# Gate rows as one-hots in pairs of tokens: one VectorE comparison for two keys, scaled copies on ScalarE

## The chip, the cores and the metric

The kernel runs on one core of a Trainium2 chip. The metric is the device time of one execution in microseconds; the median of three runs is compared. A second number, the span, is the time from the first to the last instruction in one profiled execution.

## The reference, cut to what matters

The program is a transformer block on 256 tokens of width 1024 with convolution, window attention and a "peer" layer, and after it two more layers with attention and feed-forward parts. The change lies in the peer layer alone:

```python
s_top, i_top = lax.top_k(sc, PEER_TOPK)              # 8 heads, two key sets of 128, top 16 of each
...
best, pos = lax.top_k(cand, PEER_TOPK)               # 16 of the 256 pairs, for each head
expert_idx = jnp.take_along_axis(cand_idx, pos, axis=-1)
gate = jax.nn.softmax(best, axis=-1).astype(h.dtype)
...
a = jax.nn.gelu(jnp.einsum("ced,cd->ce", u_emb[idx], hx), approximate=False)
return jnp.einsum("ce,ced->cd", g * a, v_emb[idx])
```

So each token has 8 x 16 = 128 experts out of 128 x 128. Expert (i, j) is row 128 i + j of two tables of 16384 rows and 1024 columns: its activation is the gelu of the row of the first table with the token, and the gate times that weighs the row of the second table.

## The kernel before, in words

The peer layer treats the tokens in two ways at the same time (`ROWS`, lines 80 to 81 of the kernel). The last 96 tokens are done by fetching rows. Each of 96 steps for a table fetches 128 rows of 4 KB by an indirect DMA on GpSimd's queue (`RowGroup.row`, L1555, six buffers `row`), and VectorE consumes the rows in its queue's order: a product with sum for the first table (`RowGroup.dot`, L1560, 96 times), a scaled addition for the second (`RowGroup.axpy`, L1568 and L1570, 96 times).

The first `N` = 160 tokens are done densely. For each of the 128 values of i, `ublock` loads a block of 512 KB of the first table (tiles `raw`, `whi` and `wlo`, a ring of ten buffers, by SyncE's queue, L966), TensorE multiplies it with the tokens (L976), and ScalarE writes the gelu into `G[j, i, token]` (two tiles of 64 i each). The gates have to be multiplied into `G`. For that `onehots` (L992 to L997) makes rows for `NT` = 4 tokens at a time: `Q` is one where the slot's j is the column, `O` where its i is; `P` and `R` are `O` times the high and the low part of the gate, in half precision. `place` (L1009) multiplies `Q` with `P` and `R` on TensorE, which gives the 128 x 128 table of gates of one token, eight matmuls for four tokens. VectorE multiplies this table into those parts of `G` that exist already (L1015); ScalarE writes it into the parts whose gelu comes later (L1017), and these are multiplied when their u block is done (L982, L984, L985).

The 40 groups begin after 48 of the 128 u blocks; between two placements stand two u blocks, and rows are stepped along at the rate of `some_rows`. When all u blocks and placements are through, the v phase takes 128 blocks of 512 KB of the second table through the same ring and multiplies them with `G` (L1064), first those of the second `G` tile. `add` puts in the rows' sums near the end.

Nobody writes down the order in which the engines' instructions stand: a scheduler places each engine's queue by its own estimate of durations and dependences, and then every engine runs its queue in order. So where a row operation, a comparison and a product stand relative to each other on VectorE is the scheduler's choice. The stage begins at about 457 us and its u phase ends at about 705 us.

In the program, two lines of the loop over groups tie the rows to the u blocks:

```python
ublock(i, 4 * done)
some_rows(rate)
```

Of the kernel before, what the change touches and what calls it, by code (L numbers as in the profile page):

```python
# [9 lines left out]
F32 = mybir.dt.float32  # L10
F32R = mybir.dt.float32r
F16 = mybir.dt.float16
I32 = mybir.dt.int32
U32 = mybir.dt.uint32
AF = mybir.ActivationFunctionType
ALU = mybir.AluOpType
# [4 lines left out]
T = 256  # L21
# [51 lines left out]
UP = 2.0  # L73

NT = 4
RG = 0
G_SCALE = 2.0 ** 15


# [6 lines left out]
class Kernel:  # L86
# [710 lines left out]
    def peer(self):  # L797
        nc, a = self.nc, self.a
# [2 lines left out]
        park = self.dr.tile([128, C, T], F32, name="park")  # L801
        nc.gpsimd.dma_start(park, x)
        hn = p2h.tile([128, C, T], F32, name="hn")
        iT = p2h.tile([128, T], F16, name="iT")
        jT = p2h.tile([128, T], F16, name="jT")

        gT = p2h.tile([128, T], F32, name="gT")
        gTh = p2h.tile([128, T], F16, name="gTh")
        gTl = p2h.tile([128, T], F16, name="gTl")
        sk = p2q.tile([128, 16, 128], F32, name="sk")  # L810
        nc.gpsimd.dma_start(sk, a["subk"])
        isel = p2t.tile([128, 2, 8, 16], F32, name="isel")
# [96 lines left out]
        for h in range(8):  # L909
            for c in range(2):  # L910
                pt = self.chunk(xs)
# [11 lines left out]
        def gates():  # L923
            nc.vector.scalar_tensor_tensor(ei, isel, float(N_KEYS), jsel, op0=ALU.mult, op1=ALU.add)
            nc.vector.tensor_tensor(ex, best, best[:, :, :, 0:1].to_broadcast([128, 2, 8, 16]), op=ALU.subtract)
            nc.scalar.activation(ex, ex, AF.Exp)
            sm = p2t.tile([128, 2, 8], F32, name="sm", bufs=1)
            nc.vector.reduce_sum(sm, ex, axis=AX.X)
            nc.vector.reciprocal(sm, sm)
            nc.vector.tensor_mul(ex, ex, sm[:, :, :, None].to_broadcast([128, 2, 8, 16]))  # L930

            def turn():
                for n, src in enumerate((isel, jsel, ex)):
                    pt = self.pp.tile([128, T], F32, name="ax", bufs=4)
                    for tt in range(2):
                        nc.tensor.transpose(pt[:, tt * 128:(tt + 1) * 128], src[:, tt].rearrange("p a b -> p (a b)"), self.ident)
                    nc.scalar.activation((iT, jT, gT)[n], pt, AF.Copy, scale=(1.0, 1.0, G_SCALE)[n])
                self.split(gT, gTh, gT)
                nc.scalar.activation(gTl, gT, AF.Copy)
                for g in rows:  # L940
                    g.indices()
            self.later(1, turn)
# [43 lines left out]

        def onehots(t0, oh, io):

            ts = slice(t0, t0 + NT)
            Q, O, P, R = (oh.tile([128, 128, NT], F16, name=n, bufs=2) for n in ("Q", "O", "P", "R"))  # L990
            col = lambda v: v[:, None, ts].to_broadcast([128, 128, NT])
            nc.vector.tensor_tensor(Q, io, col(jT), op=ALU.is_equal)  # L992
            nc.vector.tensor_tensor(O, io, col(iT), op=ALU.is_equal)
            nc.vector.tensor_mul(P, O, col(gTh))
            if t0 >= RG:
                for k in range(NT):
                    nc.scalar.activation(R[:, :, k], O[:, :, k], AF.Copy, scale=gT[:, t0 + k:t0 + k + 1])  # L997
            else:
                nc.vector.tensor_mul(R, O, col(gTl))
            return Q, (P, R)  # L1000

        def place(t0, n_i, oh):

# [2 lines left out]
            for t in range(4):  # L1006
                for P in Ps:
                    k = (t0 + t) % NT
                    nc.tensor.matmul(pt[:, t], Q[:, :, k], P[:, :, k], start=P is Ps[0], stop=P is Ps[-1])  # L1009
            for k in range(2):  # L1010
                view = Gs[k][:, :, t0:t0 + 4].rearrange("p i t -> p t i")
                n = min(max(n_i - 64 * k, 0), 64)
# [18 lines left out]
        pgb = self.open("pgb", side="right")  # L1031
        Gs.append(pgb.tile([128, 64, N], F32, name="G1"))
        poh = self.open("poh", side="left")
        io = poh.tile([128, 128, NT], F16, name="io")
        nc.vector.tensor_copy(io, self.iota[:, :, None].to_broadcast([128, 128, NT]))
        i0 = i
        n_g = N // 4
        rate = fetch_steps() / (254.0 - i0)
# [739 lines left out]
```

## Time and profile before

| | us |
|---|---|
| median of three runs | 1668.67 |
| lowest and highest | 1668.29, 1671.47 |
| profiled execution | 1673.91 |
| its span | 1672.1 |
| TensorE busy | 1594.9 (95%) |
| VectorE busy | 1142.8 (68%) |
| ScalarE busy | 637.1 (38%) |
| GpSimd busy | 347.1 (21%) |
| mean DMA rate over the span | 239 GB/s |

Busy time is the time in which an engine has an instruction under way. TensorE's matmuls are pipelined, so its share says little about how near it is to its best. PE is TensorE's matmuls, PEld its weight loads, DVE VectorE, ACT ScalarE, POOL GpSimd, SP SyncE. What sets the time in a stage is read from the waits and windows of that stage, not from shares over the whole span.

### The profile page before, as it was taken

What the parts mean: (1) busy time and instruction counts of PE and PEld (TensorE: products, weight loads), DVE (VectorE), ACT (ScalarE), POOL (GpSimd) and SP (SyncE); (2) the same over time, 40 slices, a digit from 0 to 9 for tenths busy, and PEclk for the clock granted to TensorE, in tenths of its full rate; (3) what the DMA queues carried; (4) which work ended last, traced back from release to release, by engine and by line L of the source; (5) the groups of instructions that cost most, each with busy time, mean ns of one, the idle gap of its engine ahead of it and who ended that gap; (6) DMA issues with size and microseconds to landing.
All of it is one profiled execution on the core that took longest, in us unless ns stands there. A gap on an engine that the chain in (4) does not pass through costs nothing.

```text
span 1672.1 us, 29794 instructions
## 1 busy us (share of the span) xinstructions
PE 1594.9 (95%) x11502; PEld 1504.6 (90%) x11502; DVE 1142.8 (68%) x2599; ACT 637.1 (38%) x1373; POOL 347.1 (21%) x288
## 2 busy tenths in 40 slices
PE   8989989998989899899999999999999999999998
PEld 7878979998989899899888999887999998799986
DVE  7989978898178899854544007866776557676654
ACT  4557545531233343200000005455544445555443
POOL 3734630000045454543332000100000020000000
PEclk9989989999999999899999999999999999999999
DMA  5522437576799999999999865732755677365563
GB/s 184 171 80 93 137 123 228 160 252 198 239 402 406 408 381 409 395 409 409 409 409 409 317 196 159 246 102 87 224 185 182 186 189 211 94 188 183 180 189 113
DMA packets 109388, 398.97 MB, mean 239 GB/s; under 512 B 12484, under 2 KB 12643, under 8 KB 108736
## 3 DMA queue, kind: packets, MB, share of 16 engines
q1 hardware_dynamic: 78336, 282.63, 50.0%
q0 software_dynamic: 30768, 114.39, 18.1%
q8 instruction: 90, 1.47, 0.4%
q14 instruction: 50, 0.41, 0.1%
q10 hardware_dynamic: 144, 0.07, 0.0%
HBM read 394.86 MB, written 6.11 MB: 240 GB/s over the span
## 4 chain that ended last, share of the span: by engine, by line
PE 60%; DMA 19%; DVE 17%; issue 3%; ACT 1%; POOL 1%; SPq 0%; DVEq 0%; POOLq 0%; ACTq 0%
PE mm L145 12%; PE mm L146 11%; PE mm L147 11%; PE ax L1064 9%; DMA row<-un,idx 8%; DMA raw<-vv 4%; DMA whi<-vv 4%; PE mm L976 3%; DVE junk L1560 2%; DVE ax L589 2%; PE mm L213 1%; DVE wlo L126 1%; PE mm L211 1%; PE mm L212 1%; PE ax L442 1%
## 5 line engine op out<-in xcount | busy, mean ns | idle before, releaser
L122 ACT ACTIVATE whi<-raw 128x1024 fp32r<-128x1024 f32 x275 | 290.3, 1058 | 620.1 <-DMA raw<-wst 310.0
L126 DVE TENSOR_TENSOR wlo<-raw,whi 128x1024 fp32r<-128x1024 f32 x227 | 277.3, 1223 | 187.8 <-ACT whi L122 184.3
L145 PE MATMUL mm<-xgh,whi 128*128 128x256 f32 x1064 | 304.3, 286 | 0.0
L147 PE MATMUL mm<-xgh,wlo 128*128 128x256 f32 x1064 | 301.8, 284 | 0.4 <-DVE wlo L126 0.4
L146 PE MATMUL mm<-xgl,whi 128*128 128x256 f32 x1064 | 301.4, 283 | 0.0
L145 PEld LDWEIGHTS mm<-xgh,whi 128*128 128x128 f32 x1064 | 201.9, 190 | 1.1 <-issue 0.8
L147 PEld LDWEIGHTS mm<-xgh,wlo 128*128 128x128 f32 x1064 | 201.9, 190 | 0.7 <-DVE wlo L126 0.6
L146 PEld LDWEIGHTS mm<-xgl,whi 128*128 128x128 f32 x1064 | 202.0, 190 | 0.1
L1570 DVE SCALAR_TENSOR_TENSOR acc<-row,w,acc 128x1024 f32<-128x1024 f32 x94 | 120.7, 1284 | 111.1 <-DMA row<-vv,idx 111.0
L1555 POOL DMA_INDIRECT row<-un,idx x96 | 105.5, 1099 | 277.6 <-DVE idx L1550 169.4
L1560 DVE CUSTOM_DVE_ANT_0 junk<-row,h 128x1024 f32<-128x1024 f32 x96 | 117.5, 1224 | 33.9 <-DMA row<-un,idx 32.4
L124 POOL TENSOR_TENSOR wlo<-raw,whi 128x1024 fp32r<-128x1024 f32 x48 | 115.1, 2403 | 107.8 <-ACT whi L122 105.0
L1064 PE MATMUL ax<-G,raw 128*128 128x160 f32 x832 | 125.6, 303 | 3.1 <-DMA raw<-vv 1.0
L1555 POOL DMA_INDIRECT row<-vv,idx x96 | 96.7, 1008 | 142.8 <-DVE acc L1570 123.5
L1064 PEld LDWEIGHTS ax<-G,raw 128*128 128x128 f32 x832 | 116.1, 191 | 8.1 <-DMA raw<-vv 7.7
L976 PE MATMUL mm<-hn,raw 128*128 128x160 f32 x816 | 121.6, 304 | 0.1
L976 PEld LDWEIGHTS mm<-hn,raw 128*128 128x128 f32 x816 | 116.5, 195 | 0.4 <-ACT G L984 0.3
L146 PE MATMUL mm<-hl,whi 128*128 128x256 f32 x368 | 106.8, 290 | 2.2 <-DVE hl L356 2.1
L976 PE MATMUL mm<-hn,wlo 128*128 128x160 f32 x608 | 95.3, 313 | 5.0 <-ACT G L979 5.0
L589 DVE SCALAR_TENSOR_TENSOR ax<-u,cw,ax 128x256 f32<-128x256 f32 x227 | 97.7, 481 | 0.7
L1064 PE MATMUL ax<-G,wlo 128*128 128x160 f32 x608 | 93.6, 306 | 2.2 <-DMA wlo<-vv 0.6
L976 PEld LDWEIGHTS mm<-hn,wlo 128*128 128x128 f32 x608 | 90.5, 201 | 5.2 <-ACT G L979 5.2
(435 smaller groups left out, 3358.2 us busy)
## 6 DMA issues: line engine op xcount, KB each, us to landing
raw<-wst SPq DMA_DIRECT2D x278, 512.0 KB, 3.7
raw<-vv SPq DMA_DIRECT2D x52, 512.0 KB, 15.1
raw<-ut SPq DMA_DIRECT2D x51, 512.0 KB, 6.6
whi<-ut SPq DMA_DIRECT2D x39, 512.0 KB, 6.6
wlo<-ut SPq DMA_DIRECT2D x38, 512.0 KB, 6.7
wlo<-vv SPq DMA_DIRECT2D x38, 512.0 KB, 14.9
whi<-vv SPq DMA_DIRECT2D x38, 512.0 KB, 15.5
tabr<-tabd POOLq DMA_DIRECT2D x1, 2048.0 KB, 8.3
```

Source lines behind the costliest of these rows:

```text
L122: nc.scalar.activation(hi, raw, AF.Copy)
L124: nc.gpsimd.tensor_sub(lo, raw, hi)
L126: self.pin = nc.vector.tensor_sub(lo, raw, hi)
L145: nc.tensor.matmul(pt, w[:, s], xs[0][:, k], start=first, stop=False)
L146: nc.tensor.matmul(pt, w[:, s], xs[1][:, k], start=False, stop=False)
L147: nc.tensor.matmul(pt, lo[:, s], xs[0][:, k], start=False, stop=last)
L589: nc.vector.scalar_tensor_tensor(y[:, c] if k == 30 else ps, u[:, c, k:k + T], cw[:, c, k:k + 1], ps, op0=ALU.mult, op1=ALU.add)
L976: nc.tensor.matmul(pt, raw[:, k * 128:(k + 1) * 128], hn[:, k, :N], start=(k == 0), stop=(k == C - 1))
L1064: nc.tensor.matmul(acc[d // 2][:, d % 2, :N], raw[:, d * 128:(d + 1) * 128], G(i), start=False, stop=False, skip_group_check=True)
L1555: self.k.nc.gpsimd.indirect_dma_start(t, None, table, bass.IndirectOffsetOnAxis(ap=self.idx[:, s:s + 1], axis=0))
L1560: self.k.nc.vector.tensor_tensor_reduce(junk, row, self.h, 1.0, 0.0, ALU.mult, ALU.add, self.a[:, s:s + 1])
L1570: self.k.nc.vector.scalar_tensor_tensor(self.acc, row, w, self.acc, op0=ALU.mult, op1=ALU.add)
```

## The change

The tiles for the keys become one, `jiT`, with j and i beside each other. `Q` and `O` become one tile `QO` with both, laid out by pairs of tokens, in three buffers instead of two. One VectorE comparison makes both keys of two tokens, so two comparisons of 512 elements make a group, where two comparisons and one product of 512 elements did. `P` is no longer a VectorE product: it is a scaled copy on ScalarE for each token, as `R` is; `P` is scaled by the gate itself and rounded to half precision when written, `R` by what that rounding leaves, which is now kept in single precision (`gTl`, one ScalarE copy fewer). `io` shrinks from four tokens to two, and `place` reads the new layout.

```diff
--- before.py
+++ after.py
@@ -73,7 +73,6 @@
 UP = 2.0
 
 NT = 4
-RG = 0
 G_SCALE = 2.0 ** 15
 
 
@@ -801,12 +800,12 @@
         park = self.dr.tile([128, C, T], F32, name="park")
         nc.gpsimd.dma_start(park, x)
         hn = p2h.tile([128, C, T], F32, name="hn")
-        iT = p2h.tile([128, T], F16, name="iT")
-        jT = p2h.tile([128, T], F16, name="jT")
+
+        jiT = p2h.tile([128, 2, T], F16, name="jiT")
 
         gT = p2h.tile([128, T], F32, name="gT")
         gTh = p2h.tile([128, T], F16, name="gTh")
-        gTl = p2h.tile([128, T], F16, name="gTl")
+        gTl = p2h.tile([128, T], F32, name="gTl")
         sk = p2q.tile([128, 16, 128], F32, name="sk")
         nc.gpsimd.dma_start(sk, a["subk"])
         isel = p2t.tile([128, 2, 8, 16], F32, name="isel")
@@ -934,9 +933,8 @@
                     pt = self.pp.tile([128, T], F32, name="ax", bufs=4)
                     for tt in range(2):
                         nc.tensor.transpose(pt[:, tt * 128:(tt + 1) * 128], src[:, tt].rearrange("p a b -> p (a b)"), self.ident)
-                    nc.scalar.activation((iT, jT, gT)[n], pt, AF.Copy, scale=(1.0, 1.0, G_SCALE)[n])
-                self.split(gT, gTh, gT)
-                nc.scalar.activation(gTl, gT, AF.Copy)
+                    nc.scalar.activation((jiT[:, 1], jiT[:, 0], gT)[n], pt, AF.Copy, scale=(1.0, 1.0, G_SCALE)[n])
+                self.split(gT, gTh, gTl)
                 for g in rows:
                     g.indices()
             self.later(1, turn)
@@ -986,18 +984,17 @@
 
         def onehots(t0, oh, io):
 
-            ts = slice(t0, t0 + NT)
-            Q, O, P, R = (oh.tile([128, 128, NT], F16, name=n, bufs=2) for n in ("Q", "O", "P", "R"))
-            col = lambda v: v[:, None, ts].to_broadcast([128, 128, NT])
-            nc.vector.tensor_tensor(Q, io, col(jT), op=ALU.is_equal)
-            nc.vector.tensor_tensor(O, io, col(iT), op=ALU.is_equal)
-            nc.vector.tensor_mul(P, O, col(gTh))
-            if t0 >= RG:
-                for k in range(NT):
-                    nc.scalar.activation(R[:, :, k], O[:, :, k], AF.Copy, scale=gT[:, t0 + k:t0 + k + 1])
-            else:
-                nc.vector.tensor_mul(R, O, col(gTl))
-            return Q, (P, R)
+
+            QO = oh.tile([128, 2, NT // 2, 128, 2], F16, name="QO", bufs=3)
+            P, R = (oh.tile([128, NT // 2, 128, 2], F16, name=n, bufs=2) for n in ("P", "R"))
+            for p in range(NT // 2):
+                ps = slice(t0 + 2 * p, t0 + 2 * p + 2)
+                nc.vector.tensor_tensor(QO[:, :, p], io[:, None].to_broadcast([128, 2, 128, 2]),
+                                        jiT[:, :, None, ps].to_broadcast([128, 2, 128, 2]), op=ALU.is_equal)
+            for k in range(NT):
+                for dst, g in ((P, gT), (R, gTl)):
+                    nc.scalar.activation(dst[:, k // 2, :, k % 2], QO[:, 1, k // 2, :, k % 2], AF.Copy, scale=g[:, t0 + k:t0 + k + 1])
+            return QO[:, 0], (P, R)
 
         def place(t0, n_i, oh):
 
@@ -1006,7 +1003,7 @@
             for t in range(4):
                 for P in Ps:
                     k = (t0 + t) % NT
-                    nc.tensor.matmul(pt[:, t], Q[:, :, k], P[:, :, k], start=P is Ps[0], stop=P is Ps[-1])
+                    nc.tensor.matmul(pt[:, t], Q[:, k // 2, :, k % 2], P[:, k // 2, :, k % 2], start=P is Ps[0], stop=P is Ps[-1])
             for k in range(2):
                 view = Gs[k][:, :, t0:t0 + 4].rearrange("p i t -> p t i")
                 n = min(max(n_i - 64 * k, 0), 64)
@@ -1031,8 +1028,8 @@
         pgb = self.open("pgb", side="right")
         Gs.append(pgb.tile([128, 64, N], F32, name="G1"))
         poh = self.open("poh", side="left")
-        io = poh.tile([128, 128, NT], F16, name="io")
-        nc.vector.tensor_copy(io, self.iota[:, :, None].to_broadcast([128, 128, NT]))
+        io = poh.tile([128, 128, 2], F16, name="io")
+        nc.vector.tensor_copy(io, self.iota[:, :, None].to_broadcast([128, 128, 2]))
         i0 = i
         n_g = N // 4
         rate = fetch_steps() / (254.0 - i0)
```

The instructions stand in other places too. The first place is VectorE's queue in the middle of the stage, between the product of one group and that of the next (`G<-ax,G`; `ISA junk` is the product with sum of one fetched row, `ISA a` the short read of its sum). Before:

```order
L1015 SCALAR_TENSOR_TENSOR G_5136<-ax,G_5136 128x4x26
L992 TENSOR_TENSOR Q<-io,jT 128x512
L994 TENSOR_TENSOR P<-O,gTh 128x512
L1560 ISA junk,a_4056<-row,h_4052 128x1024
L1560 ISA a_4056 128x1
L985 TENSOR_TENSOR G_5136<-G_5136,ac 128x88
L993 TENSOR_TENSOR O<-io,iT 128x512
L1560 ISA junk,a_4056<-row,h_4052 128x1024
L1560 ISA a_4056 128x1
L1560 ISA junk,a_4056<-row,h_4052 128x1024
L1560 ISA a_4056 128x1
L985 TENSOR_TENSOR G_5136<-G_5136,ac 128x88
```

With the change, the same group:

```order
L1012 SCALAR_TENSOR_TENSOR G_5134<-ax,G_5134 128x4x26
L992 TENSOR_TENSOR QO<-io,jiT 128x2x256 x2
L1557 ISA junk,a_4065<-row,h_4061 128x1024
L1557 ISA a_4065 128x1
L983 TENSOR_TENSOR G_5134<-G_5134,ac 128x88
L1560 TENSOR_TENSOR w_4056<-w_4056,gate_4054 128x64
L1557 ISA junk,a_4065<-row,h_4061 128x1024
L1557 ISA a_4065 128x1
L1557 ISA junk,a_4065<-row,h_4061 128x1024
L1557 ISA a_4065 128x1
L983 TENSOR_TENSOR G_5134<-G_5134,ac 128x88
L1012 SCALAR_TENSOR_TENSOR G_4047<-ax,G_4047 128x4x64
```

The product `P` and the comparison `O` are gone from between the rows; the two comparisons that stand behind the product belong to the group three further on, where `Q` and `P` belonged to the next one. Three row products stand in the group in both.

The second place is ScalarE's queue in the same stage, from one copy of the gate table (`G<-ax`) to the next. Before:

```order
L1017 ACTIVATE G_5136<-ax 128x4x59
L982 ACTIVATE ac<-mm 128x44
L984 ACTIVATE G_5136<-mm 128x116
L982 ACTIVATE ac<-mm 128x44
L984 ACTIVATE G_5136<-mm 128x116
L997 ACTIVATE R<-O,gT 128x128 x4
L1017 ACTIVATE G_5136<-ax 128x4x57
```

With the change:

```order
L1014 ACTIVATE G_5134<-ax 128x4x55
L996 ACTIVATE R<-QO,gTl 128x128
L996 ACTIVATE P<-QO,gT 128x128
L996 ACTIVATE R<-QO,gTl 128x128
L980 ACTIVATE ac<-mm 128x52
L982 ACTIVATE G_5134<-mm 128x108
L980 ACTIVATE ac<-mm 128x52
L982 ACTIVATE G_5134<-mm 128x108
L996 ACTIVATE P<-QO,gT 128x128
L996 ACTIVATE R<-QO,gTl 128x128
L996 ACTIVATE P<-QO,gT 128x128
L996 ACTIVATE R<-QO,gTl 128x128
```

Four scaled copies between two such table copies have become eight; three of them stand between the table copy and the gelu of the next u blocks (`ac<-mm` and `G<-mm`).

The third place is VectorE's queue at the end of the u phase, from the last product on (`acc<-row` is the scaled addition of one row of the second table). Before:

```order
L1015 SCALAR_TENSOR_TENSOR G_4048<-ax,G_4048 128x4x64
L1015 SCALAR_TENSOR_TENSOR G_5136<-ax,G_5136 128x4x62
L1570 SCALAR_TENSOR_TENSOR acc_4053<-row,w_4057,acc_4053 128x1024
L985 TENSOR_TENSOR G_5136<-G_5136,ac 128x160
L1570 SCALAR_TENSOR_TENSOR acc_4053<-row,w_4057,acc_4053 128x1024 x2
L985 TENSOR_TENSOR G_5136<-G_5136,ac 128x160
L1570 SCALAR_TENSOR_TENSOR acc_4053<-row,w_4057,acc_4053 128x1024 x51
L1568 TENSOR_SCALAR acc_4063<-row,w_4067 128x1024
L1570 SCALAR_TENSOR_TENSOR acc_4063<-row,w_4067,acc_4063 128x1024 x31
```

With the change:

```order
L1012 SCALAR_TENSOR_TENSOR G_4047<-ax,G_4047 128x4x64
L1012 SCALAR_TENSOR_TENSOR G_5134<-ax,G_5134 128x4x62
L1567 SCALAR_TENSOR_TENSOR acc_4052<-row,w_4056,acc_4052 128x1024
L983 TENSOR_TENSOR G_5134<-G_5134,ac 128x160
L1567 SCALAR_TENSOR_TENSOR acc_4052<-row,w_4056,acc_4052 128x1024 x2
L983 TENSOR_TENSOR G_5134<-G_5134,ac 128x160
L1567 SCALAR_TENSOR_TENSOR acc_4052<-row,w_4056,acc_4052 128x1024 x41
L1565 TENSOR_SCALAR acc_4062<-row,w_4066 128x1024
L1567 SCALAR_TENSOR_TENSOR acc_4062<-row,w_4066,acc_4062 128x1024 x31
```

Behind the last product stand 1 + 2 + 51 + 1 + 31 = 86 row operations before and 1 + 2 + 41 + 1 + 31 = 76 with the change, so of the 192 there are 106 ahead of it before and 116 with the change. The queues of SyncE and GpSimd have the same order in both.

## Rows read from the trace of the kernel before

**Rows 1.** The page's slices of 41.8 us: busy tenths, DMA share, rate.

```profile
...
DVE  7989978898178899854544007866776557676654
...
DMA  5522437576799999999999865732755677365563
GB/s 184 171 80 93 137 123 228 160 252 198 239 402 406 408 381 409 395 409 409 409 409 409 317 196 159 246 102 87 224 185 182 186 189 211 94 188 183 180 189 113
```

**Rows 2.** Windows of the peer stage; the first row names the columns.

```profile
core 0: us, PE busy (x) PEld busy (x) DVE busy (x) ACT busy (x) POOL busy (x), PEclk, DMA share, GB/s
457.00:705.00 248.00, 223.02 (x1601) 219.00 (x1599) 210.88 (x476) 90.56 (x366) 122.45 (x111) 0.96 1.01 399
457.00:490.00 33.00, 32.66 (x247) 32.14 (x246) 23.52 (x55) 14.24 (x52) 15.11 (x17) 1.00 0.99 386
490.00:580.00 90.00, 77.71 (x553) 75.97 (x552) 74.18 (x175) 33.36 (x131) 44.47 (x41) 0.96 1.03 407
580.00:610.00 30.00, 27.30 (x190) 27.29 (x191) 29.37 (x71) 13.46 (x53) 16.00 (x14) 0.89 0.97 370
610.00:670.00 60.00, 56.97 (x418) 56.40 (x418) 53.07 (x121) 21.47 (x90) 29.10 (x26) 0.97 1.03 409
670.00:705.00 35.00, 28.37 (x199) 27.21 (x197) 30.73 (x57) 8.03 (x40) 17.77 (x15) 0.94 1.01 395
705.00:791.00 86.00, 85.87 (x609) 85.67 (x609) 44.02 (x36) 0.48 (x3) 35.18 (x36) 0.96 1.02 408
791.00:924.00 133.00, 125.43 (x824) 113.03 (x823) 64.97 (x51) 0.00 (x0) 44.38 (x47) 1.00 1.03 409
924.00:1013.00 89.00, 89.00 (x666) 89.00 (x664) 7.60 (x14) 6.32 (x14) 0.00 (x0) 1.00 0.66 224
```

**Rows 3.** Waits, 457 to 705 us: us in total, times, longest.

```profile
ACT G L1017 <- DVE G L1015: 149.9, 40, 5.9
DVE junk L1560 <- DMA row<-un,idx: 32.4, 33, 2.4
PE ax L1009 <- DVE P L994: 21.5, 13, 4.4
PEld L1009 <- DVE Q L992: 20.2, 12, 4.3
```

**Rows 4.** Timeline, weight loads and VectorE: start, length, instruction, idle before.

```profile
...
579.90 1.22 DVE L1560 CUSTOM_DVE_ANT_0 junk<-row,h 128x1024 f32<-128x1024 f32 x1 [1.40 <-DMA row<-un,idx]
...
582.37 0.12 PEld L1009 LDWEIGHTS <-Q 128*128 128x128 f16 x1 [4.29 <-DVE Q L992]
...
600.74 0.94 PEld L1009 LDWEIGHTS <-Q 128*128 128x128 f16 x8
...
606.03 0.94 PEld L1009 LDWEIGHTS <-Q 128*128 128x128 f16 x8
```

**Rows 5.** Waits, 705 to 924 us.

```profile
PEld ax L1064 <- DMA raw<-vv: 7.7, 20, 1.0
PEld ax L1064 <- DMA wlo<-vv: 5.9, 15, 0.9
PEld ax L1064 <- DMA whi<-vv: 5.7, 15, 0.7
```

**Rows 6.** Groups by shape, 457 to 705 us: busy us, mean ns, idle before.

```profile
L997 ACT ACTIVATE R<-O,gT 128x128 f16<-128x128 f16 x160 | 63.0, 585 | 1.8 <-DVE O L993 1.8
L992 DVE TENSOR_TENSOR Q<-io,jT 128x512 f16<-128x512 f16 x40 | 16.8, 420 | 0.0
L1560 DVE CUSTOM_DVE_ANT_0 junk<-row,h 128x1024 f32<-128x1024 f32 x96 | 117.5, 1224 | 33.9 <-DMA row<-un,idx 32.4 <-DVE O L993 0.5
L985 DVE TENSOR_TENSOR G<-G,ac 128x156 f32<-128x156 f32 x2 | 0.6, 318 | 0.0
```

**Rows 7.** Tile G: ns min/median/max, first and last start, shapes.

```profile
L985 DVE TENSOR_TENSOR G<-G,ac x79: 158/248/321, 465.2 to 711.0; 128x4 f32<-128x4 f32 x2, 128x8 f32<-128x8 f32 x2, 128x12 f32<-128x12 f32 x2, 128x16 f32<-128x16 f32 x2
```

**Rows 8.** Timeline, ScalarE: four copies in a row.

```profile
662.43 1.50 ACT L997 ACTIVATE R<-O,gT 128x128 f16<-128x128 f16 x4
```

## The prediction

> **What bounds the kernel now.** I read the page's slices first, then the stretch around the change window by window, then its waits, then single rows. In the slices [rows 1] the DMA digit is 9 from the twelfth slice to the twenty-second (460 to 920 us), at about 400 GB/s or more, and VectorE is at 7 to 9 in the first half of that and at 4 to 5 after. That stretch holds two phases. In the u phase, which the change touches, TensorE makes 80 of the 128 u blocks (512 KB each) and 40 groups of four tokens are placed; in the v phase it runs through 128 v blocks. Beside both, GpSimd fetches 192 gathered rows (96 of each table, 128 partitions x 4 KB, so 512 KB as well), which VectorE consumes in its queue's order.
>
> The windows [rows 2] say what limits the u phase. The DMA engines move 407 and 409 GB/s in its two long middle windows, and 408 to 409 in the v phase as long as rows are left. The mix of blocks and rows differs between the phases; the rate does not. So I take 409 GB/s as what this traffic can have: 1.28 us for each 512 KB. Over 457 to 705 us the mean is 399, so 248 x 10/409 = 6.1 us of that phase were not used. The moved 399 x 248 = 98.95 MB are 188.7 pieces of 0.524 MB: 80 blocks and about 108 rows. 188.7 x 1.28 = 242 us, and 6 unused, make the 248. **The phase ends when its rows have landed**, not when TensorE could be done.
>
> The waits [rows 3] fit: VectorE waits 32.4 us for rows, 33 times, and is busy for 210.9 of the other time [rows 2]; TensorE waits 20.2 us for a Q and 21.5 us for a P, which are the same stops (its weight load and its matmul) and are VectorE's queue being late. Where nothing is late, placements follow each other in 5.29 us [rows 4], 40 x 5.29 = 212 us; the rest of the 248 is these stops and the clock after them (granted 0.89 of full speed on average in the worst window [rows 2], so for a part of it the lower level, 1.2 GHz). The worst stop, 4.29 us to 582.37 [rows 4], ends behind a row operation of VectorE that waited 1.40 us for a row [rows 4], and the window of 580 to 610 us moved only 370 GB/s: with TensorE stopped, no block buffer came free and only rows were asked for.
>
> After 705 us, TensorE first lives on the blocks that are loaded ahead; from 791 to 924 it waits for nearly each block, 7.7 + 5.9 + 5.7 = 19.3 us in 50 waits, 0.39 us each [rows 5], and VectorE takes 51 rows in 133 us, 2.6 us a row. When the rows are through (924 us) TensorE runs without a wait. Fewer rows left for the v phase shorten that starved stretch.
>
> **The change, part by part.**
>
> VectorE's own work. Removed: 40 Q, 40 O and 40 P of one shape at 0.42 us [rows 6], 50.4 us. Added: 80 comparisons of the same 512 half-precision elements, whose inner run is two instead of four. No row shows runs of two. From below 0.42 us each, as Q now; from above, an operation without the double rate: the product G<-G,ac goes from 158 ns at 4 elements to 318 at 156 [rows 6, 7], 1.05 ns an element, so 512 would take 158 + 508 x 1.05 = 0.69 us. I take 0.42, the row of the same operation, type and count. Net -16.8 us busy; +4.8 at the other end (80 x 0.27 = 21.6 more). Cover: VectorE waits for rows anyway, and what it saves becomes a longer wait for rows. So -16.8 us of work is worth nothing by itself.
>
> VectorE's order. This is the part that I price. The order before has 106 row operations ahead of the last product G<-ax,G, the changed one has 116 (the third place of the order shown: 86 left behind it, now 76), because the scheduler fills the lighter queue with rows. The v phase cannot begin until that product is done, since its first blocks read that tile. Ten more rows must land before: **10 x 1.28 = +12.8 us**.
>
> Lookahead. QO has three buffers and both comparisons of a group stand right behind the product of three groups before; ScalarE's copies run about one and a half groups ahead. So a place waits no longer for a Q behind rows of its own group, but for the product two groups earlier: TensorE may run one group (5.3 us) ahead of VectorE. That absorbs single late rows such as the 4.29 us stop, keeps block buffers coming free, and fills the hole of 580 to 610 us: 30 x 39/409 = 2.9 us. The other unused time (1.9 us at the start, where the first rows are under way; 1.2 at the end) stays. **-2.9 us**, between 0 and all 6.1. The 20.2 us of Q waits don't go: TensorE has 212 us of work in a phase whose transfers take over 250, and its waits come back as waits for copies or for the last product.
>
> The v phase. Ten rows fewer there: 26 us less of the starved stretch at 2.6 us a row, 10 blocks that don't wait 0.39 us: **-3.9 us**; 0 to -3.9, since more than the waits of those blocks cannot go.
>
> ScalarE. 160 more copies. Four take 1.50 us in a row [rows 8], one alone 0.585 [rows 6], so one more costs 0.305: +49 us, at most 160 x 0.585 = 94 us, on an engine busy for 90.6 of 248 us [rows 2]: 140 to 184. The cover is its 149.9 us of waits for the product [rows 3]. Behind that wait now stand copies too: a place two groups on needs the first two or three of them, some 1.2 us after the product. With TensorE a group ahead that costs nothing; if the lead is gone, it is 1.2 us against the Q and P (two at 0.42) that it waits for now, 0.4 us at 13 stops, 5 us at most. The Trainium skill's page "ScalarE: Activation LUTs", section "Rules for kernel authors", says that multiplications belong on VectorE rather than ScalarE. No row contradicts it on the price; what it would make of the sum is the fourth rival.
>
> Once each: the first placement needs eight copies behind its comparisons, 2.7 us against 1.5, against one small copy (gTl, 0.42) that goes; both lie under two u blocks that are already loaded. TensorE's 320 placement matmuls stay the same in number; their step in memory halves (two elements instead of four), which its waits cover in either direction.
>
> Sum: 12.8 - 2.9 - 3.9 = **+6.0 us**. The profiled execution took 1673.91 us (span 1672.1, 1.8 around it), 5.2 above the median of 1668.67; the difference is put on the median: **1674.7 us**. With the recovery between 6.1 and 0 this case reaches from 1671.6 to 1677.6; without the v phase's part, 1681.5.
>
> **The rivals.**
>
> 1. *The holes fill.* All 6.1 us are recovered because TensorE's lead keeps both streams asking all the time: 12.8 - 6.1 - 3.9 = +2.8, 1671.5 us, within 0.2% (3.3 us, about what a measurement of this kernel can tell from no change). For it: the middle windows are at 407 to 409 already. Against: the start and the end of the phase have few requests whatever the order. Decided by a mean of 407 GB/s or more from 457 us to the first v block.
>
> 2. *Faster.* The 409 GB/s are no limit but what the present waits let through, and VectorE's queue is the pacer: then Q's 20.2 us go, 1648.5 us. For it: VectorE is busy or waiting for rows nearly throughout, and the change takes 16.8 us from it and uncouples TensorE. Against: the same 408 to 409 in both phases with different mixes. It decides if rates above 415 GB/s show. The Trainium skill's page "DMA: Bandwidth & Descriptors", section "Where 436 GB/s comes from", gives 435 GB/s as the fabric's ceiling; by that the 198.7 pieces would take an estimated 239.5 us, less than the phase takes now, and the kernel would gain. The windows here never show it.
>
> 3. *Slower by VectorE.* The comparisons in pairs lose the double rate: 210.9 - 16.8 + 21.6 + 12.6 (ten rows at 1.22 busy and a short read) = 228 us busy, 17.4 more on an engine that is busy or waiting for rows for 243 of 248 us: +17.4 - 3.9 = +13.5, 1682.2 us. For it: no row shows runs of two. Against: type, operation and count are as in Q. It decides at 0.6 us and more for a QO.
>
> 4. *Slower by ScalarE.* Each place waits for its copies: 40 x (1.22 for four more copies - 0.42 for the P that goes) = +32, 1701 us. Against: even at 0.585 a copy, eight copies, four gelu pieces and the copy of the product make some 6 us a group, under the 6.3 that the transfers ask (2 blocks and 2.9 rows).
>
> **Chances.** The forecast 0.52, the filled holes 0.21, faster 0.12, VectorE 0.12, ScalarE 0.03. Slower by over 0.2%: 0.52 + 0.12 + 0.03 = 0.67; same 0.21; faster 0.12. The range from 1666 to 1685 holds the forecast with its bounds, the first rival and most of the third; it leaves out the second, the fourth and a corner of the third, some 0.19.
>
> **What would show it.** Right: QO at about 0.42 us, 80 of them; VectorE some 4 us less busy up to the last product (10 rows more, 16.8 us less) and waiting 40 us or more for rows; 407 to 409 GB/s in the u phase's middle; the first v block 8 to 12 us later than 705; some 40 waits for v blocks instead of 50; ScalarE at 140 to 185 us in the phase. The waits of TensorE for a Q are gone, and others, for P, R or the last product, of the same size stand in their place. Wrong: a v phase that begins at 705 or earlier, or a DMA rate well off 409.

## The result, and the profile after

The changed kernel took 1682.03 us (median of 5 runs, 1679.01 to 1684.99), the kernel before 1669.06 in the same rounds: **ratio 1.0074, 95% interval 1.0055 to 1.0094**, 13.0 us slower. The forecast was slower, 1674.7 us, with a range of 1666 to 1685. So the direction and the range held, and the sum was too small: +6.0 was worked out and +13.0 came. The profiled execution took 1684.99 us, span 1683.2, which is 11.1 more than the span before. One execution of one kernel below (e10) took 3940 us; it is left out of that kernel's median, and its trace is not read.

The windows of the changed kernel, same columns as in [rows 2]; the u phase now ends near 722 us and the rows near 913, and the last line is the u phase as a whole:

```profile
457.00:490.00 33.00, 29.24 (x231) 27.88 (x230) 22.84 (x56) 18.93 (x74) 17.27 (x17) 1.00 0.96 372
490.00:580.00 90.00, 77.69 (x546) 72.19 (x546) 70.92 (x162) 44.95 (x181) 47.59 (x42) 0.94 1.03 406
580.00:610.00 30.00, 24.86 (x185) 23.60 (x185) 25.01 (x59) 15.83 (x64) 18.31 (x13) 0.94 1.01 390
610.00:670.00 60.00, 51.18 (x377) 47.24 (x376) 49.34 (x110) 29.26 (x123) 31.04 (x27) 0.97 1.03 406
670.00:705.00 35.00, 32.31 (x238) 30.72 (x238) 31.50 (x55) 18.05 (x78) 21.67 (x17) 0.95 1.02 405
705.00:721.80 16.80, 6.64 (x39) 5.26 (x38) 11.51 (x16) 2.08 (x14) 7.30 (x7) 0.74 1.01 399
721.80:800.00 78.20, 77.99 (x552) 77.41 (x553) 40.84 (x34) 0.22 (x2) 31.73 (x33) 0.97 1.00 393
800.00:913.00 113.00, 106.44 (x700) 95.88 (x699) 54.98 (x45) 0.00 (x0) 36.80 (x39) 1.00 1.03 409
913.00:1027.00 114.00, 114.00 (x849) 114.00 (x850) 7.31 (x14) 6.69 (x15) 0.00 (x0) 1.00 0.70 226
457.00:721.80 264.80, 221.91 (x1612) 206.89 (x1610) 211.12 (x453) 129.09 (x528) 143.19 (x122) 0.94 1.01 399
```

Read against [rows 2], three things stand out. The long middle windows move 406 GB/s, as before (407 and 409), and the mean of the phase is 399 as before, over 264.8 us instead of 248: **more was moved at the same rate**, 105.7 MB against 98.95, which is 12.8 pieces of 512 KB more. Which they are is read from the DMA queues of the u phase (packets, MB, share of 16 engines; q0 has GpSimd's rows, q1 SyncE's blocks). Before, 457 to 705 us:

```profile
q0 software_dynamic: 15428, 56.19, 57.5%
q1 hardware_dynamic: 11634, 42.37, 43.3%
```

With the change, 457 to 721.8 us:

```profile
q0 software_dynamic: 17262, 62.88, 60.2%
q1 hardware_dynamic: 11693, 42.55, 40.8%
```

The blocks are the same but for 0.18 MB; the rows are 6.69 MB more, 12.8 rows. Ten of them are the ten rows ahead of the last product; nearly three more had landed, and were not used yet, when the phase ended. The hole of 580 to 610 us is half filled (370 to 390). And there is a new stretch, 705 to 721.8, in which TensorE is busy for 6.64 of 16.8 us, at a mean granted clock of 0.74 of full speed.

The two marks by which I measure the phase are the first issue of a gathered row and the first matmul on the finished tile G (tile views: name, count, ns min/median/max, first and last start):

```profile
L1552 POOL DMA_INDIRECT row<-un,idx x96: 939/946/2471, 457.4 to 662.6; - x96
...
L1061 PE MATMUL ax<-G,wlo x608: 299/299/474, 722.3 to 1025.9; 128*128 128x160 f32 x152
```

The u phase by these marks is 722.3 - 457.4 = 264.9 us; before it was 705.7 - 456.1 = 249.6. The v phase, to the start of its last matmul, is 1026.4 - 722.3 = 304.1 against 1012.8 - 705.7 = 307.1. So the profile's 11.1 us are +15.3 in the u phase, -3.0 in the v phase, +1.3 because the stage begins later, and -2.5 behind it.

The waits of the u phase, as in [rows 3]:

```profile
ACT G L1014 <- DVE G L1012: 122.5, 35, 8.6
...
DVE junk L1557 <- DMA row<-un,idx: 39.6, 38, 2.1
PEld L1006 <- issue: 27.5, 39, 4.9
...
PE ax L1006 <- ACT R L996: 12.9, 7, 4.7
...
PEld ax L1066 <- ACT G L1014: 6.5, 1, 6.5
...
PE ax L1006 <- ACT P L996: 6.2, 5, 2.1
```

VectorE waits for rows 39.6 us instead of 32.4. TensorE hardly waits for VectorE's keys any more (0.6 us at its weight loads); it waits for ScalarE's R and P and, once and long, for the last product (L1066 prepares the sums of the v phase; L1014, ScalarE's write of the rest of the last table of gates, stands between the two and waits for VectorE's product). For 27.5 us of waits of the placements' weight loads the profile names no releaser. The names have changed, the stops have not gone.

The instructions that the change touches, grouped by shape (busy us, mean ns, idle before):

```profile
L996 ACT ACTIVATE P<-QO,gT 128x128 f16<-128x128 f16 x160 | 71.2, 445 | 0.8 <-DVE QO L992 0.8
L996 ACT ACTIVATE R<-QO,gTl 128x128 f16<-128x128 f16 x160 | 70.4, 440 | 0.0
...
L992 DVE TENSOR_TENSOR QO<-io,jiT 128x512 f16<-128x512 f16 x80 | 30.3, 428 | 0.0
...
L1006 PE MATMUL ax<-R,QO 128*128 128x128 f16 x160 | 27.2, 219 | 21.6 <-ACT R L996 12.9 <-ACT ac L980 5.6 <-issue 0.8
...
L1006 PEld LDWEIGHTS <-QO 128*128 128x128 f16 x320 | 23.5, 97 | 30.0 <-issue 27.5 <-DVE QO L992 0.6
```

A comparison with runs of two takes 428 ns where Q took 420 [rows 6]: the rate is kept. A copy takes 440 to 445 ns where it took 585 [rows 6].

### The profile page after: what moved, and what is told of

The parts are those of the page before. It is cut to its first block, busy times and chain, and to the rows that moved or that the text cites. A ratio compares the mean times of both kernels' runs of the same rounds, so it can differ in the third digit from the quotient of the medians.

```text
span 1683.2 us, 29938 instructions
## 1 busy us (share of the span) xinstructions
PE 1588.9 (94%) x11502; PEld 1489.5 (88%) x11502; DVE 1128.6 (67%) x2559; ACT 674.8 (40%) x1532; POOL 356.0 (21%) x288
## 3 DMA queue, kind: packets, MB, share of 16 engines
q1 hardware_dynamic: 78336, 282.63, 50.4%
## 4 chain that ended last, share of the span: by engine, by line
PE 60%; DMA 19%; DVE 15%; issue 3%; ACT 1%; POOL 1%; SPq 0%; DVEq 0%; POOLq 0%; ACTq 0%
PE mm L144 12%; PE mm L145 11%; PE mm L146 11%; PE ax L1061 10%; DMA row<-un,idx 9%; PE mm L974 4%; DMA raw<-vv 4%; DMA whi<-vv 2%; DMA row<-vv,idx 2%; DVE ax L588 2%; PE mm L212 2%; PE mm L210 1%; PE mm L211 1%; PE ax L441 1%; DVE wlo L125 1%
## 5 line engine op out<-in xcount | busy, mean ns | idle before, releaser
L1552 POOL DMA_INDIRECT row<-un,idx x96 | 110.4, 1150 | 265.7 <-DVE idx L1547 169.9
L1557 DVE CUSTOM_DVE_ANT_0 junk<-row,h 128x1024 f32<-128x1024 f32 x96 | 117.9, 1228 | 44.7 <-DMA row<-un,idx 39.6
L1552 POOL DMA_INDIRECT row<-vv,idx x96 | 100.7, 1049 | 134.6 <-DVE acc L1567 107.9
L974 PEld LDWEIGHTS mm<-hn,whi 128*128 128x128 f32 x624 | 89.8, 196 | 7.8 <-issue 4.2
```

Of the source, the lines that this page charges most:

```text
L974: nc.tensor.matmul(pt, raw[:, k * 128:(k + 1) * 128], hn[:, k, :N], start=(k == 0), stop=(k == C - 1))
L1552: self.k.nc.gpsimd.indirect_dma_start(t, None, table, bass.IndirectOffsetOnAxis(ap=self.idx[:, s:s + 1], axis=0))
L1557: self.k.nc.vector.tensor_tensor_reduce(junk, row, self.h, 1.0, 0.0, ALU.mult, ALU.add, self.a[:, s:s + 1])
```

## The experiments

**The theory**: the phase lasts as long as its transfers, and what sets their number is how many of the 192 row operations stand ahead of the last product in VectorE's queue (106 before, 116 after). **Rival A**: ScalarE's copies of P delay the placements. **Rival B**: the comparisons in pairs, with operands two elements apart, cost the time. The first two kernels undo or do one part of the change and let the scheduler order the rest. All the others leave every instruction as it is and set the count: each product is remembered, each row operation may not be issued ahead of the latest product (an ordering edge, which adds no work), and the rate at which rows are handed out gives the count.

```diff
+        self.prod = []
...
-                next(fetch, None)
+                with self.tc.issue_after(self.prod[-1].ins) if self.prod else nullcontext():
+                    next(fetch, None)
...
-        rate = fetch_steps() / (254.0 - i0)
+        rate = 111.01 / (126.0 - i0)
...
+        rate = (fetch_steps() - 111.0) / 125.0
```

These are the edits for 106 rows; 111 is that count and 5, since the first five steps only start fetches. The edges set the count and the even spread; the scheduler orders the other queues anew around them. In e8, e4 and e9, 9, 19 and 8 of the 40 places are split up on TensorE between matmuls of u blocks; in the two kernels themselves it is one. What came out, with the two kernels themselves; u and v phases by the marks above, from each kernel's trace. Each ratio is to the kernel before in the same rounds, whose median lay between 1669.06 and 1671.80 us:

| kernel | rows ahead | u phase, us | v phase, us | median, us | ratio to before (95%) |
|---|---|---|---|---|---|
| before | 106 | 249.6 | 307.1 | 1669.06 | 1 |
| changed | 116 | 264.9 | 304.1 | 1682.03 | 1.0074 (1.0055 to 1.0094) |
| e1 changed, P on VectorE | 105 | 253.2 | 306.2 | 1675.44 | 1.0034 (1.0022 to 1.0046) |
| e2 before, P on ScalarE | 115 | 260.6 | 302.8 | 1678.21 | 1.0048 (1.0032 to 1.0064) |
| e3 changed, even | 106 | 247.9 | 305.9 | 1670.20 | 0.9999 (0.9989 to 1.0008) |
| e4 before, even | 115 | 260.7 | 303.4 | 1677.54 | 1.0047 (1.0032 to 1.0063) |
| e5 changed, even | 85 | 221.4 | 314.7 | 1650.56 | 0.9873 (0.9857 to 0.9888) |
| e6 changed, even | 70 | 196.5 | 332.3 | 1645.73 | 0.9849 (0.9832 to 0.9865) |
| e7 before, even | 85 | 220.9 | 313.5 | 1649.43 | 0.9870 (0.9855 to 0.9885) |
| e8 before, even | 106 | 247.4 | 306.1 | 1669.76 | 0.9993 (0.9984 to 1.0002) |
| e9 changed, even | 115 | 257.9 | 302.0 | 1675.60 | 1.0031 (1.0019 to 1.0043) |
| e10 before, even | 70 | not read | not read | 1654.41 | 0.9900 (0.9885 to 0.9914) |
| e11 changed, even | 60 | 198.0 | 342.3 | 1653.92 | 0.9899 (0.9886 to 0.9912) |
| e12 before, even | 70 | 213.1 | 327.1 | 1655.86 | 0.9921 (0.9908 to 0.9935) |

**e1. P back on VectorE.**

```diff
-                for dst, g in ((P, gT), (R, gTl)):
-                    nc.scalar.activation(dst[:, k // 2, :, k % 2], ...
+            nc.vector.tensor_mul(P, QO[:, 1], col)
...
+                nc.scalar.activation(R[:, k // 2, :, k % 2], ...
```

> The changed kernel with one part undone: P is again one VectorE product of the one-hot rows with the gates' upper halves; R stays a scaled copy on ScalarE, the comparisons in pairs stay. The scheduler then puts 105 row operations ahead of the last product instead of 116. Theory (rows ahead of the last product set the end of the u phase, 1.28 us each): v phase begins near 707 us, 11 to 14 us earlier than in the changed kernel (721.8), time 1669 to 1672 us, ratio to before 1.000 to 1.002. Rival A (ScalarE's copies of P delay the placements): also near 1669 us, so this run alone does not separate the two; the third and fourth do. Rival B (the pairs themselves, operands two elements apart, cost the time): stays near 1682 us.

Somewhat over half of the loss went, not all: the ratio lies above what the theory allowed. The trace has a likely reason in the last 40 us: from 670 to 695 us only 347 GB/s are moved, VectorE waits 5.59 us for the first row of the second table, and eight row operations stand between the last comparison and the last product, one of which waits 2.53 us. With one row fewer than e3 the u phase is 5.3 us longer, so this order of the scheduler costs a few us beyond its count; which part of it does was not tried.

**e2. P on ScalarE in the kernel before.**

```diff
-            nc.vector.tensor_mul(P, O, col(gTh))
+            for k in range(NT):
+                nc.scalar.activation(P[:, :, k], O[:, :, k], AF.Copy, scale=gT[:, t0 + k:t0 + k + 1])
...
```

> The kernel before with one part of the change alone: P as four scaled copies a group on ScalarE, Q and O as before, four tokens in one comparison. The scheduler puts 115 row operations ahead of the last product instead of 106. Theory: v phase begins 9 x 1.28 = 11.5 us or more later than 705 us, time 1677 to 1683 us, ratio 1.005 to 1.009. Rival A (ScalarE's copies delay the placements; here at 585 ns instead of 445): 1682 us or above, and ScalarE without long waits. Rival B (the pairs cost the time): near 1669 us.

This part of the change (with R scaled by the low part of the gate in single precision, as there), and the comparisons of four tokens as they were, make the kernel before 0.48% slower. So the pairs of rival B are not needed for a loss; whether they add to it, e3 shows. Rival A is not yet told apart, since the edit also moves the count to 115.

**e3. The changed kernel, 106 rows ahead.**

> The changed kernel in every instruction, only VectorE's queue is held to 106 row operations ahead of the last product, as many as in the kernel before (86 behind it), by ordering edges from the products to the rows. Theory: v phase begins 10 to 13 x 1.28 us earlier than 721.8, at 705 to 710 us; time 1668 to 1672 us, ratio 0.999 to 1.002. Rival A (ScalarE's copies delay the placements) and rival B (the pairs): stays near 1682 us, ratio 1.006 or more, because neither the copies nor the pairs are touched.

Every instruction of the change is there, with its copies and its pairs, and the loss is gone: 0.9999. Both rivals fall. TensorE still waits for ScalarE's P and R in this kernel (5.9 and 9.0 us); the time of the program doesn't depend on it.

**e4. The kernel before, 115 rows ahead.**

> The kernel before in every instruction, only with 115 row operations ahead of the last product instead of 106, by ordering edges alone. Theory: v phase begins 11 to 15 us later than 705, time 1677 to 1684 us, ratio 1.005 to 1.009: as slow as the changed kernel without any of its edits. Rivals A and B: near 1669 us, ratio 1.000 to 1.002.

The counterpart: no edit of the change, only nine rows moved, and the kernel before is as slow as with P on ScalarE (260.7 and 260.6 us of u phase, 1.0047 and 1.0048).

**e5. The changed kernel, 85 rows ahead.**

> The changed kernel with 85 row operations ahead of the last product and 107 behind it, by ordering edges alone. Theory: 21 rows fewer than in the run with 106 take 21 x 1.28 = 27 us from the u phase, v phase begins near 680 us if TensorE keeps up; the v phase gets longer by 0.4 to 0.5 us a row (measured so far: 9 or 10 rows fewer there made it 3.0 to 4.3 us shorter), 8 to 11 us. Net -16 to -19: time 1651 to 1655 us, ratio 0.989 to 0.992, faster than both kernels. Rival (beyond 106 rows something else ends the u phase, TensorE with its copies): v phase at 700 us or later, 1668 us or above.

Predicted from the count alone, and met in kind: v phase at 678.6 us, 1650.56 us, a little below what was expected (0.9873 against 0.989 to 0.992). The 21 rows fewer take 247.9 - 221.4 = 26.5 us from the u phase, **1.26 us a row**, and give 8.8 back in the v phase, 0.42 a row.

**e6. The changed kernel, 70 rows ahead.**

> The changed kernel with 70 row operations ahead of the last product, 122 behind. Theory: (80 + 70 + 3) x 1.28 us is 196 us of transfers, less than TensorE's 200 to 212 us of work in the phase, so the end of the u phase is TensorE's: v phase at 665 to 675 us; the v phase has rows nearly to its end and grows by 15 to 18 us against 106 rows. Time 1644 to 1652 us, ratio 0.984 to 0.989. Rival (85 is already past the balance, the v phase starves throughout): 1655 us or above.

1645.73 us: 1.5% faster than the kernel before and the fastest of all that were run. The time lies in the expected range by two misses that offset each other: the v phase grew by 26.4 us against 106 rows, where 15 to 18 were expected, and it begins at 652.3 us, earlier than expected, since TensorE's own work in the phase is 195 us and not the 200 to 212 that I took:

```profile
457.00:652.00 195.00, 194.86 (x1598) 192.79 (x1598) 159.76 (x376) 136.08 (x526) 85.60 (x77) 1.00 1.02 402
```

TensorE (first column behind the length) is busy for 194.86 of 195.00 us at full granted clock, while the transfers still run at 402 GB/s: at this count the two limits meet.

**e7. The kernel before, 85 rows ahead.**

> The kernel before in every instruction with 85 row operations ahead of the last product, by ordering edges alone. Theory: as the changed kernel with 85, near 1651 to 1657 us, ratio 0.989 to 0.993; if it is later, the difference between the two at equal rows is what the change itself is worth (places of 0.94 instead of 0.58 us, P on VectorE). Rival (the pairs and copies of the change are what lets rows move): 1665 us or above.

0.9870 beside 0.9873, both a little faster than expected: at 85 rows, as at 106, the two kernels take the same time. Nothing of the gain at 85 rows needs the change.

**e8. The kernel before, 106 rows ahead, even.**

> A control: the kernel before with 106 row operations ahead of the last product as the scheduler gave it, but spread evenly over the products by the same ordering edges as in the other runs. Theory (the count decides, the edges and the even spread cost or give little): 1667 to 1672 us, ratio 0.998 to 1.001. If the edges themselves give time: ratio 0.997 or below, and the run of the changed kernel with 106 rows owes its time to them in part. If they cost time: 1.002 or above.

0.9993, its interval across 1: the edges and the even spread by themselves are worth at most 0.0016 x 1670 = 2.7 us. Against e7 the 21 rows are again 247.4 - 220.9 = 26.5 us, 1.26 a row.

**e9. The changed kernel, 115 rows ahead, even.**

> A control for the changed kernel: as many row operations ahead of the last product as the scheduler gave it (115 of 116), but spread evenly over the products by the ordering edges. If the count alone decides: as the kernel before with 115, 1676 to 1680 us, ratio 1.004 to 1.006. If the changed kernel's own instructions cost 4 to 6 us more when many rows are ahead: 1681 to 1684 us, ratio 1.007 to 1.009. In the first case what the changed kernel lost beyond its count, about 5 us, is the uneven order of its rows.

The first case, and a little below it: 1.0031, clear of the changed kernel's interval. With the same instructions and a count one lower, it is 0.0043 x 1669 = 7.2 us faster; less the 1.26 us of that row, the order is worth some 6 us. Where it lies is read from VectorE's timeline (start, length, instruction, idle before). In the changed kernel, from the last comparison to the last product:

```profile
698.87 0.76 DVE L992 TENSOR_TENSOR QO<-io,jiT 128x512 f16<-128x512 f16 x2
699.54 1.29 DVE L1567 SCALAR_TENSOR_TENSOR acc<-row,w,acc 128x1024 f32<-128x1024 f32 x1
...
701.53 1.28 DVE L1567 SCALAR_TENSOR_TENSOR acc<-row,w,acc 128x1024 f32<-128x1024 f32 x1 [0.48 <-DMA row<-vv,idx]
...
702.96 1.16 DVE L1012 SCALAR_TENSOR_TENSOR G<-ax,G 128x256 f32<-128x256 f32 x2
704.09 1.28 DVE L1567 SCALAR_TENSOR_TENSOR acc<-row,w,acc 128x1024 f32<-128x1024 f32 x1
707.11 1.28 DVE L1567 SCALAR_TENSOR_TENSOR acc<-row,w,acc 128x1024 f32<-128x1024 f32 x1 [1.73 <-DMA row<-vv,idx]
...
709.67 1.28 DVE L1567 SCALAR_TENSOR_TENSOR acc<-row,w,acc 128x1024 f32<-128x1024 f32 x1 [1.05 <-DMA row<-vv,idx]
...
712.23 1.28 DVE L1567 SCALAR_TENSOR_TENSOR acc<-row,w,acc 128x1024 f32<-128x1024 f32 x1 [1.05 <-DMA row<-vv,idx]
713.43 1.10 DVE L1012 SCALAR_TENSOR_TENSOR G<-ax,G 128x256 f32<-128x256 f32 x2
714.80 1.28 DVE L1567 SCALAR_TENSOR_TENSOR acc<-row,w,acc 128x1024 f32<-128x1024 f32 x1 [0.27 <-DMA row<-vv,idx]
...
717.36 2.72 DVE L1567 SCALAR_TENSOR_TENSOR acc<-row,w,acc 128x1024 f32<-128x1024 f32 x2 [1.04 <-DMA row<-vv,idx]
...
720.23 1.11 DVE L1012 SCALAR_TENSOR_TENSOR G<-ax,G 128x256 f32<-128x256 f32 x2
```

And in e9:

```profile
705.95 0.76 DVE L994 TENSOR_TENSOR QO<-io,jiT 128x512 f16<-128x512 f16 x2
...
706.85 1.28 DVE L1570 SCALAR_TENSOR_TENSOR acc<-row,w,acc 128x1024 f32<-128x1024 f32 x1
...
708.27 1.28 DVE L1570 SCALAR_TENSOR_TENSOR acc<-row,w,acc 128x1024 f32<-128x1024 f32 x1
709.47 0.66 DVE L1014 SCALAR_TENSOR_TENSOR G<-ax,G 128x256 f32<-128x256 f32 x1
710.02 1.29 DVE L1570 SCALAR_TENSOR_TENSOR acc<-row,w,acc 128x1024 f32<-128x1024 f32 x1
711.22 0.67 DVE L1014 SCALAR_TENSOR_TENSOR G<-ax,G 128x248 f32<-128x248 f32 x1
```

Nine rows stand between the last comparison and the last product in the changed kernel, three in e9. TensorE's weight loads at the same place, in the changed kernel:

```profile
704.40 0.71 PEld L1006 LDWEIGHTS <-QO 128*128 128x128 f16 x7
705.30 0.10 PEld L1006 LDWEIGHTS <-QO 128*128 128x128 f16 x1 [0.20 <-issue]
...
714.87 0.29 PEld L1066 LDWEIGHTS ax<-zeros,zero 128*128 128x128 f32 x1 [4.43 <-issue]
721.67 0.29 PEld L1066 LDWEIGHTS ax<-zeros,zero 128*128 128x128 f32 x1 [6.51 <-ACT G L1014]
```

The last placement's loads end at 705.4 us in the changed kernel, and the product that ends it is 15 us behind, with six rows between, which VectorE waits for 1.73 + 1.05 + 1.05 + 0.27 + 1.04 = 5.14 us. Meanwhile SyncE loads v blocks ahead, which share the transfers with these rows (2.38 of the 7.16 MB from 704 to 722 us). In e9 the last placement (709.2 us) and the last product lie 2 us apart.

**e10 and e12. The kernel before, 70 rows ahead.**

> The kernel before with 70 row operations ahead of the last product. In the changed kernel TensorE is busy for all of the u phase at 70 rows (195.2 of 195.3 us). Theory: here the edit itself counts, since a place of eight matmuls takes 0.94 us instead of 0.58: 40 x 0.36 = 14 us more TensorE work in a phase that is TensorE's; v phase begins near 665 us instead of 652.3, some of it given back in the v phase, time 1650 to 1660 us, ratio 0.987 to 0.993. Rival (equal rows give equal times here too, as at 106 and 85): 1644 to 1648 us, ratio 0.984 to 0.986.

1654.41 us, as the theory had it. For its trace the kernel was run once more.

> The kernel before with 70 rows ahead once more, for its trace. If the edit's shorter places are what it lacks against the changed kernel with 70 rows (1655.0 against 1645.7 us so far): TensorE busy for 99% or more of the time from 457 us to the v phase, which begins at 663 to 668 us (652.3 in the changed kernel), matmuls of the places at 296 ns, no row that TensorE waits for. If rows or ScalarE hold it instead: TensorE idle for 5 us or more before the v phase, with P, Q or R named behind its waits.

1655.86 us; the v phase begins at 668.9 us, 16.6 after that of e6, of which the 40 places x 0.36 us account for 14:

```profile
457.00:662.00 205.00, 204.76 (x1550) 203.25 (x1549) 171.62 (x406) 100.25 (x361) 81.04 (x74) 1.00 1.00 383
```

TensorE is busy for 204.76 of 205.00 us and the transfers fall to 383 GB/s. **Here the phase is TensorE's, and only here does the change pay**: 0.9849 against 0.9900 and 0.9921 at equal rows, 8 to 12 us.

**e11. The changed kernel, 60 rows ahead.**

> The changed kernel with 60 row operations ahead of the last product. Theory: TensorE ends the u phase already at 70 rows, so the u phase gets no shorter (v phase at 650 to 653 us), and ten more rows in the v phase cost it 0.5 to 1.2 us each: 1650 to 1658 us, slower than with 70. Rival (fewer rows ahead go on paying): 1640 us or below.

1653.92 us: the u phase is 198.0 us (196.5 with 70), the v phase grows by 10.0 us for ten rows. Of the counts tried 70 is the best for the changed kernel and 85 for the kernel before; nothing between 60 and 70 or between 70 and 85 was tried. Best beside best, the change is worth little: 0.9849 (1645.73 us) against 0.9870 (1649.43 us), with intervals that overlap.

## Why the prediction was right, and where its sum failed

The cause and the direction were forecast, and the mechanism held in its main term. That the range held 1682.03 us is luck: the forecast's own bounds ended at 1677.6, and the room above was there for the third rival and for a v phase that gives nothing back, neither of which came. The first v block was to come 8 to 12 us later and came 16.6 later (722.3 beside 705.7).

**What bounds the phase: right.** The transfers did, at the rate of [rows 2], and the time went with the number of rows ahead of the last product. The runs make a row 1.26 us twice (e3 to e5, e8 to e7; 21 rows each), where the forecast had 1.28. Over the nine rows from 106 to 115 it is 1.11 (e3 to e9) and 1.48 (e8 to e4), 11 to 15 us for ten rows; why these two differ is open.

**VectorE's order, +12.8: right** in kind and size. That nothing else in the change costs or gives time at these counts is shown by e3 and e8 (0.9999 and 0.9993) and by e5 and e7.

**Lookahead, -2.9: this is the step that failed.** The premise was that TensorE's lead of one group would absorb late rows and fill the hole of 580 to 610 us. The hole was half filled (390 GB/s), but the mean of the phase stayed at 399, 265 x 10/409 = 6.5 us unused as before (6.1): nothing was recovered, so the first rival falls as well. At equal, even counts the lead recovers nothing either. From 457 us to the v phase e3 moved 398 GB/s and e8, without the lead, 401; e9 moved 405 and e4, without it, 404.

The forecast followed the lead through the middle of the phase and not to its end. A comparison that is issued three groups ahead leaves its rows between it and its own group's product, and at the end of the phase there is no further group to hide them: TensorE is through early and stands until the last product, 4.43 + 6.51 us in the changed kernel, where it was 3.88 us in the kernel before and is 0.60 us in e9. That order beyond the count costs some 6 us is shown by e9; that it is this tail is read from the timelines and was not tried by moving the tail alone, and e9 has other places on TensorE split up too.

**Rows fetched ahead: a term that was left out.** The sum counted the ten rows that must be used before the phase ends, and not those that land before it ends. By the queues above, nearly three rows more than before had landed unused, 2.8 x 1.28 = 3.5 us by an estimate at the rate of the phase. With the 12.8 of the ten rows that is 16.3 of the 16.8 us by which the phase from 457 us on got longer. Ten v blocks are issued ahead in both kernels, the tenth at 710.45 us in the changed one; the next is issued at 726.77 us, so in the last part of the tail rows alone are asked for. Behind the last product VectorE then takes seven rows without waiting for one, where in the kernel before it waits 2.03 us for the second. These rows are not paid back in the v phase, which got no shorter than ten rows were to make it.

**The v phase, -3.9: -3.0** in the profile. TensorE waited for v blocks 19.3 us before [rows 5]; now 4.6 + 3.1 + 2.9 = 10.6 in 26 waits are named so, and 7.1 in 20 more name no releaser. From 106 to 85 rows it is 0.42 and 0.35 us a row, as the 0.39 that was used; below 85 it is more, 1.17 from 85 to 70 and 1.00 from 70 to 60 (e5, e6, e11).

**VectorE's own work: right.** Comparisons and products went from 50.4 us to 30.3 (two comparisons in a row take 0.76 us), somewhat more than the 16.8 that was taken off, and came back as waits for rows: 39.6 instead of 32.4. Worth nothing, as was said. The third rival, that the pairs lose the double rate, would have given 1682.2 us, which is the time that came; the row of 428 ns refutes it all the same. A time that fits is no evidence for its mechanism.

**ScalarE: cover right, price too high.** 160 more copies were to cost 49 to 94 us; the engine's busy time went from 90.6 to 129.1, 38.5 more, since each copy became shorter. The fourth rival, that the placements wait for their copies, falls with e3. The Trainium skill's page "ScalarE: Activation LUTs", section "Rules for kernel authors", would have these multiplications on VectorE. On the price of one the trace of e1 agrees: a product for four tokens takes 426 ns on VectorE, and a copy for one token 443 ns on ScalarE. With P back there (e1) the kernel gained, but by the rows that its order moved behind the last product; at equal rows (e3 beside e8) it makes no difference that these runs can tell.

**The second rival**, a rate above 409, never showed: no slice of a page (some 41 us) moves more than 410 GB/s. The Trainium skill's page "DMA: Bandwidth & Descriptors", section "Where 436 GB/s comes from", gives 435 GB/s for the fabric and about 358 for what one core's loads from HBM are bound by. The 409 of these traces, with one core at work, lies between: the first is not reached here by either order, and the second is exceeded.

## What to carry to other kernels

In a stage that its transfers bound, ask of every change how many of the optional transfers its new instruction order puts ahead of the operation that ends the stage; here that count alone moved the changed kernel from 1645.7 us (70 rows) to 1675.6 (115), and the edits themselves, at 85 and 106 rows, gave nothing while the transfers were the bound. When an engine gets a lead, follow it to the end of the stage, where there is nothing left to run ahead of. And when a scheduler fills a lighter queue with background work, set that amount by hand: count the transfers that fit under the other engine's work (here 70 rows and 80 blocks under 195 us of TensorE) and leave the rest to the next stage.

## What the runs showed of the hardware that was not expected

The step between elements of the placement operands went from four halves to two, and with it both engines that read them became quicker (no run changed the step alone). A weight load of 128x128 halves takes 97 ns instead of 116, its matmul 219 instead of 297. A place of eight weight loads takes 0.58 us instead of the 0.94 of [rows 4]:

```profile
601.26 0.58 PEld L1006 LDWEIGHTS <-QO 128*128 128x128 f16 x8
...
606.12 0.58 PEld L1006 LDWEIGHTS <-QO 128*128 128x128 f16 x8
```

ScalarE's scaled copy of 128x128 halves takes 440 to 445 ns instead of 585. Neither is worth anything that these runs can tell at 85 or 106 rows (e7 beside e5, e8 beside e3); at 70, where TensorE is the bound, the shorter places are what makes the changed kernel the faster of the two.
